# A two-layer decoder trunk on one core: the second layer's first gate moved into round 1, T's products put on both sides of the Gram products, and other moves of order

## The chip, the core and the metric

The kernel runs on one core of a Trainium2 chip. The core has a matrix engine (TensorE, PE), whose weight loads are listed apart (PEld), a vector engine (VectorE, DVE), a scalar engine (ScalarE, ACT), GpSimd (POOL) and SyncE (SP). Each runs its own program in order, and they wait for each other through semaphores. SP and POOL issue most of the DMA transfers, so a transfer that must wait for its buffer holds up those behind it on the same queue. The metric is the device time of one execution in microseconds.

## The reference

A 512 × 2048 fp32 input goes through two residual layers, each `x + W_out(mixer(RMSNorm(x)) * silu(gate))`.

Layer 0 is differential attention with 8 heads: `q, k, v, gate = split(h @ w_in)`; q and k are normalised and rotated; two softmax maps are subtracted (`a = p0 - lam * p1`); `o = a @ v` is normalised, gated and projected.

Layer 1 is RWKV-7 with 32 heads of 64 channels. A projection, mixed with its shift by one token, gives r, k, v, the gate and two low-rank terms for decay and learning rate. Each head then runs the scan

```
sa = S @ a_t
S  = S * w_t + sa b_t^T + v_t k_t^T
y  = S @ r_t
```

and y is normalised per head, gets a bonus term, is gated and projected.

## The kernel before

All large products are made from fp32r pairs: a float is split into a high and a low part (`split_w`: ACT casts the high part wh at L105, DVE subtracts to get the low part wl at L106), and each product is three matmuls (hH·wh, hL·wh, hH·wl). A unit of 48 such matmuls projects one block of columns. Almost all of PE's time is in these units (tile pp).

**Layer 0.** Head 0 uses `unit_tok`, heads 1 to 7 `unit_head`, a scheme with sums of blocks as in Strassen's method. The sums of weights are made by the DMA: `add_w` (L83) loads a weight block into a tile that holds another and adds it, on POOL's queue. The groups S1, S2, S3, S4 are products with sums of the activations; `all_groups` walks through one of them, splits each weight tile (wraw, or Ta to Td), issues its matmuls, and asks for the next sum in the same tile. b22 are the weight tiles that S4 loads and S3 uses; in the last head they are loaded in `third`, behind S2. Attention for head h−1 is a `Chain`: a generator of small steps that moves on by "ticks", one for each projection product issued. So its score, value and transposing products (sc, o, yt at L391) lie between head h's projections. The constants of layer 1 (`rwkv_consts`) are a chain too, put behind head 1, ahead of the attention chain in head 2. Then the out-projection follows, two column blocks by `unit_tok`, the rest by sums.

**Layer 1.** There are 16 rounds j, each for 128 channels (two heads). A round has units for k (with stage1), r (stage2), v (stage_v) and, from round 3, the gate of round j−3 (`LAG = 3`). Time is cut into 8 chunks of 64 tokens. In each round:

- `gram` (L1279) forms the products between keys and receptances of each chunk (gp, L1290), copies them to G on ACT (L1297), sums squares over channels (L1209, L1210, copy ssl at L1302), and sends both to DRAM (ltd, L1304 and L1310, on SP). `mask_gram` masks G on POOL.
- `t_solve` (L1335) loads them back as LT (POOL's queue, L1344), solves a triangular system in 31 pairs of DVE steps (L1355, L1357, end L1358), and writes td (L1359, SP).
- The chain of round j−1 runs among the units of round j. `t_combine` (L1366) loads TT from td (L1372), transposes it on DVE (T, L1382), and makes two products, px(T,G) (L1388) and, with the copy X between them (L1391), px(TT,X) (L1398). `scan_pair` then goes through the 8 chunks, with three dependent products each (sm at L1469, L1480, L1487) and copies on ACT between them (rhs L1472, VS L1482). After them come the outputs Y (L1509, L1513) and their centring.
- Later rounds finish: group norm, bonus, gate.

How far apart a chain's steps lie is written by hand in ticks: `GAP_D`, `GAP_X`, `GAP_T` in `t_combine`, and `gap`, `gap_s` in `scan_pair`. In round j > 2 `gram` moves the chain on by one step (`before.step`) right behind its own products. The rest of the order comes from a scheduler which sorts each engine's instructions by priorities (`AHEAD`, `SCAN`, `SOLVE` are offsets). After round 15 the last chain runs among the gates 13, 14, 15 and the out-projection of layer 1.

Of the kernel before, what the change touches and what calls it, by code (L numbers as in the profile page):

```python
# [82 lines left out]
def add_w(g, raw, part, k0):  # L83

    w, c = part
    g.nc.gpsimd.dma_start(out=raw[:], in_=w[c][:, k0 : k0 + KG], accum_op=ALU.add)

# [75 lines left out]
def unit_tok(g, aH, aL, parts, cols, npp=NT, more=None, late=True, turn=None, behind=None):  # L163

    nc = g.nc
    pts = [g.pp.tile([P, 512], F32, name="pp", tag="pp") if t < npp else
           g.ps.tile([P, 512], F32, name="pt", tag="pb", bufs=2) for t in range(NT)]
# [363 lines left out]
def unit_head(g, aps, h, t1s, sq, turned):  # L531
# [39 lines left out]

    def all_groups(out, lhs, raw, start=False, end=False, then=None):
        for i in range(N):
            r = raw(i)
            products(out, lhs(i), r, start and i == 0, end and i == N - 1)
            if then:
                add_w(g, r, then[0], then[1] + i * KG)

# [32 lines left out]
    def third():  # L611
        for i in range(N):
            if last:
                with g.tc.issue_after(behind):
                    b22.append(load(i, NH4, c2))
                add_w(g, b22[i], c2, i * KG)
            products(y, form("S3", i), b22[i], end=i == N - 1)
# [178 lines left out]
def layer0(g, aps):  # L796
# [3 lines left out]
    with ExitStack() as cx:  # L800
# [91 lines left out]
        for h in range(NH):  # L892
# [13 lines left out]
            if h:  # L906
                values = unit_head(g, aps, h, t1s, sq, lambda: Chain(g, keys(2), 9))
            else:
# [15 lines left out]
            if h == 1:  # L924
                Chain(g, rwkv_consts(g, aps))
                g.chains[0].step(g)
        rows = []
        for k in range(KT - 2):
            rows.append([g.hp.tile([P, T], F32R, name=n, tag=n) for n in ("hH", "hL")])
            for x, d in zip(rows[k], g.ys):  # L930
                nc.sync.dma_start(out=x[:].bitcast(F32), in_=d[k * P : (k + 1) * P, :])
        ch = Chain(g, attention(g, h, *before, 20, rows, rest), 16)
# [9 lines left out]
        def new_x(cb):  # L942
            xq = g.work.tile([P, NT, 512], F32, name="xq", tag=("sA", "sB", "qkL", "qkT")[cb], bufs=1)
            for t in range(NT):
                (nc.gpsimd if cb < 2 else nc.sync).dma_start(out=xq[:, t, :], in_=aps["x"][0, t * P : (t + 1) * P, cb * 512 : cb * 512 + 512])
            xs.append(xq)
            return xq
# [245 lines left out]

LAG = 3

# [83 lines left out]
def gram(g, j, p, before):  # L1279

    nc, w, BK = g.nc, g.work, p.BK
    p.G = w.tile([P, NC_, 2, 2, C], F32, name="G1", tag="G1", bufs=2)
    p.BKT = w.tile([P, NC_, P], F32, name="BKT", tag="BKT", bufs=2)
# [11 lines left out]
    for c0, gp in halves:  # L1295
        for h in range(2):
            nc.scalar.copy(p.G[:, c0 : c0 + 4, :, h, :], gp[h][:].rearrange("p (u x t) -> p u x t", u=4, x=2))  # L1297
    ps = g.ps.tile([P, 512], F32, name="pt", tag="pb", bufs=2)
    sum_channels(g, ps[:2, :], g.ones[:, 0 : P : C], p.k2)
    ss = w.tile([2, T], F32, name="ssl", tag="thg", bufs=1)  # L1300
    with g.tc.high_priority(offset=SOLVE if j == D // P - 1 else 0):
        nc.scalar.copy(ss[:], ps[:2, :])  # L1302
        for half in range(2):
            nc.sync.dma_start(  # L1304
                out=g.ltd[j % 2, half, :, :, HALF, :],
                in_=ss[:].rearrange("h (c b t) -> h c b t", c=NC_, b=2)[:, :, half, :])
        for half in range(2):
# [54 lines left out]

GAP_D, GAP_X, GAP_T = 18, 19, 8


def t_combine(g, j, p):  # L1366

# [9 lines left out]
    px = g.ps.tile([P, 512], F32, name="px", tag="pd", bufs=1)  # L1377
    yield GAP_D - GAP_T
    for h in range(2):
# [68 lines left out]

def chain(g, j, p, delay, gap, gap_s, others=()):
    def steps():  # L1450
        yield from t_combine(g, j, p)
        yield from scan_pair(g, j, p, gap, gap_s, dict(others))
# [100 lines left out]
def layer1(g, aps):  # L1553
    nc, tc = g.nc, g.tc
    with ExitStack() as cx:
# [17 lines left out]
        def receptances(j):  # L1573
            return shift_mix(g, proj(0, j), P, *mus(g, 0, j), "r", 1)

        begin(0)
# [43 lines left out]
        gps = proj(3, j - 1)  # L1620
# [139 lines left out]
```

## Time and profile before

| | |
|---|---|
| runs | 2126.84, 2135.11, 2135.95 us, median 2135.11 |
| the profiled execution | 2131.0 us, of which the span is 2129.3 |
| PE busy | 2091.2 us, 98% |
| DVE, ACT, POOL busy | 76%, 54%, 17% |
| mean granted PE clock | 0.996 |
| a steady round of layer 1 | 61.9 us |
| a steady head of layer 0 | 89.0 us |

The span is what the trace covers. A line of waits reads: engine, instruction and its line, what it waited for; total us, times, longest. A line of a timeline reads: start and length in us, engine, line, operation, tiles, shapes, count, and in brackets the idle time before it and what ended it. The granted clock is the share of its full rate at which the throttle let PE run.

### The profile page before, as it was taken

Reading aid. Unit: us, or ns where it says so; the run is one execution under the profiler, and the core shown is the slowest. Engines: PE = TensorE matmul, PEld = TensorE weight load, DVE = VectorE, ACT = ScalarE, POOL = GpSimd, SP = SyncE. Lnnn points to the kernel's source line nnn. Section 1 sums busy time; section 2 is a strip of 40 time slices with the busy share of each in tenths; the row PEclk is TensorE's granted clock in tenths of the full one; section 3 lists DMA queues with packets and bytes.
Section 4 is the critical chain, followed back from the end, with each engine's and each line's share of the span. In section 5 each row is a group of like instructions: output and inputs, shape, how many; then the busy total and the mean of one; then the engine's idle time right before and its main releaser. Section 6 shows DMA issues by size and latency. Waiting matters only on the chain.

```text
span 2129.3 us, 34082 instructions
## 1 busy us (share of the span) xinstructions
PE 2091.2 (98%) x11852; PEld 1690.3 (79%) x11852; DVE 1613.0 (76%) x4129; ACT 1155.5 (54%) x2278; POOL 367.9 (17%) x735
## 2 busy tenths in 40 slices
PE   9999999999999999999999999999999999999999
PEld 7888788888887788878677877778777777877787
DVE  6987888888888875576677777887777788776645
ACT  5765556566565543355555555555555555545322
POOL 1021111102113000101222221222222122231101
PEclk9999999999999999999999999999999999999999
DMA  8587878879789936722222332332333333345565
GB/s 266 161 166 186 161 167 186 164 189 172 178 183 215 314 113 179 150 90 88 78 74 84 98 91 84 93 91 77 94 103 88 84 91 92 107 134 178 173 171 121
DMA packets 158972, 294.60 MB, mean 138 GB/s; under 512 B 64352, under 2 KB 81760, under 8 KB 158800
## 3 DMA queue, kind: packets, MB, share of 16 engines
q1 hardware_dynamic: 109696, 182.82, 27.7%
q0 software_dynamic: 24448, 85.64, 22.0%
q10 hardware_dynamic: 24656, 23.97, 3.4%
q8 instruction: 93, 1.52, 0.3%
q14 instruction: 79, 0.65, 0.1%
HBM read 268.71 MB, written 23.66 MB: 137 GB/s over the span
## 4 chain that ended last, share of the span: by engine, by line
PE 77%; DVE 10%; ACT 6%; issue 3%; DMA 3%; ACTq 0%; POOL 0%; SPq 0%; DVEq 0%; POOLq 0%
PE pp L122 36%; PE pp L567 21%; PE pt L122 4%; DVE wl L106 3%; ACT wh L105 1%; PE gp L1290 1%; PE sc L122 1%; PE sm L1480 1%; PE sm L1469 1%; PE sm L1487 1%; PE o L122 1%; DVE tmpl L1355 1%; ACT VS L1427 1%; PE lora L122 1%; PE z L122 1%
## 5 line engine op out<-in xcount | busy, mean ns | idle before, releaser
L106 DVE TENSOR_TENSOR wl<-wraw,wh 128x1024 fp32r<-128x1024 f32 (+2 forms) x291 | 360.4, 1239 | 257.5 <-ACT wh L105 249.7
L105 ACT CAST wh<-wraw 128x1024 fp32r<-128x1024 f32 (+2 forms) x291 | 303.8, 1044 | 296.9 <-PE pp L122 130.3
L122 PE MATMUL pp<-hH,wl 128*128 128x512 f32 x1024 | 415.1, 405 | 0.0
L122 PE MATMUL pp<-hH,wh 128*128 128x512 f32 x1024 | 414.4, 405 | 0.0
L122 PE MATMUL pp<-hL,wh 128*128 128x512 f32 x1024 | 413.1, 403 | 0.0
L122 PEld LDWEIGHTS pp<-hH,wh 128*128 128x128 f32 x1024 | 193.7, 189 | 34.7 <-issue 0.6
L122 PEld LDWEIGHTS pp<-hL,wh 128*128 128x128 f32 x1024 | 193.9, 189 | 34.4
L122 PEld LDWEIGHTS pp<-hH,wl 128*128 128x128 f32 x1024 | 193.8, 189 | 34.0
L567 PE MATMUL pp<-wh,hH 128*128 128x512 f32 x448 | 177.8, 397 | 0.8 <-DVE G L528 0.8
L567 PE MATMUL pp<-wh,hL 128*128 128x512 f32 x448 | 176.8, 395 | 0.0
L122 PE MATMUL pp<-wh,hH 128*128 128x512 f32 x372 | 145.8, 392 | 3.9 <-ACT hH L1091 1.6
L122 PE MATMUL pp<-wl,hH 128*128 128x512 f32 x372 | 146.3, 393 | 0.4 <-DVE wl L106 0.4
L122 PE MATMUL pp<-wh,hL 128*128 128x512 f32 x372 | 146.0, 393 | 0.3 <-DVE hL L1092 0.2
L1355 DVE SCALAR_TENSOR_TENSOR tmpl<-LT,Tm 128x60 f32<-128x60 f32 (+24 forms) x496 | 134.7, 272 | 12.1
L567 PE MATMUL pp<-wl,hH 128*128 128x512 f32 x448 | 141.2, 394 | 1.3 <-DVE wl L106 1.3
L1475 POOL COPY SA<-VS 64x64 f32<-64x64 f32 x224 | 57.7, 257 | 466.6 <-DVE VS L1491 399.8
L1357 DVE TENSOR_TENSOR Tm<-Tm,tmpl 128x60 f32<-128x60 f32 (+24 forms) x496 | 103.6, 209 | 10.0 <-DVE tmpl L1355 0.2
L1472 ACT COPY rhs<-sm 64x64 f32<-64x64 f32 x256 | 53.0, 207 | 99.9 <-PE sm L1469 97.4
L567 PEld LDWEIGHTS pp<-wl,hH 128*128 128x128 f32 x448 | 84.8, 190 | 19.4 <-DVE wl L106 2.1
L567 PEld LDWEIGHTS pp<-wh,hH 128*128 128x128 f32 x448 | 84.7, 189 | 18.6 <-DVE G L528 1.2
L567 PEld LDWEIGHTS pp<-wh,hL 128*128 128x128 f32 x448 | 84.8, 189 | 16.4
L122 PEld LDWEIGHTS pp<-wh,hH 128*128 128x128 f32 x372 | 69.9, 188 | 19.6 <-ACT hH L1091 2.6
(393 smaller groups left out, 4426.5 us busy)
## 6 DMA issues: line engine op xcount, KB each, us to landing
wraw<-in_rw_w_in_dram SPq DMA_DIRECT2D x128, 512.0 KB, 3.9
wraw<-in_da_w_in_dram SPq DMA_DIRECT2D x75, 512.0 KB, 3.5
wraw<-in_da_w_in_dram POOLq DMA_DIRECT2D x28, 512.0 KB, 6.1
wraw<-in_da_w_out_dram SPq DMA_DIRECT2D x26, 512.0 KB, 4.5
wraw<-in_rw_w_out_dram SPq DMA_DIRECT2D x26, 512.0 KB, 4.5
Ta<-in_da_w_in_dram POOLq DMA_DIRECT2D x21, 512.0 KB, 5.9
Tb<-in_da_w_in_dram POOLq DMA_DIRECT2D x21, 512.0 KB, 5.8
Tc<-in_da_w_in_dram POOLq DMA_DIRECT2D x21, 512.0 KB, 5.8
```

What stands on the lines that cost most here:

```text
L105: a = nc.scalar.copy(hi[:, ks], raw[:, ks])
L106: d = nc.vector.tensor_sub(lo[:, ks], raw[:, ks], hi[:, ks].bitcast(F32))
L122: m = nc.tensor.matmul(out, a, b, start=s, stop=e, skip_group_check=skip)
L567: m = nc.tensor.matmul(out[t][:], x, wt[lo][:, k, :], start=first, stop=end and lo == 1 and k == KG - 1, skip_group_check=True)
L1290: m = nc.tensor.matmul(gp[h][:, i * P : (i + 1) * P], BK[r_, c0 + i, :, :], p.AR[r_, c0 + i, :, :], start=True, stop=True)
L1355: nc.vector.scalar_tensor_tensor(tt, LT[:, i : i + 1, i + 1 :].to_broadcast([P, s, n]), n2[:, i : i + 1], Tm[:, 0:s, i : i + 1].to_broadca ...
L1357: nc.vector.tensor_add(Tm[:, 0:s, i + 1 :], Tm[:, 0:s, i + 1 :], tt)
L1427: nc.scalar.copy(p.VS[(1 - h) * C : (2 - h) * C, par : NC_ : 2, h, :], pv[par * C : par * C + C, :, h, :])
L1469: nc.tensor.matmul(sm[:, 0:P], both(p.G[:, c, 0]), both(VS[:, c]), start=True, stop=True)
L1472: nc.scalar.copy(rhs[r_, :], sm[r_, h * C : h * C + C])
L1475: nc.gpsimd.tensor_copy(p.SA[r_, c - 1, :], VS[r_, c, h, :])
L1480: nc.tensor.matmul(sm[:, P : P + C], both(g.TT[j % 2][:, c]), rhs[:], start=True, stop=True)
```

## The change

1. `LAG` goes from 3 to 2. Gate 0 is computed in round 1, in a tile of its own (tag g0), and applied at the end of round 2; later gates come one round sooner; after the loop gates 14 and 15 are left.
2. In `gram` the channel sums, their copy and their two transfers go ahead of the Gram products, with the `SOLVE` offset in every round, and in another bank.
3. `GAP_X` goes from 19 to 10. From round 4 on, with `before.step` from j > LAG + 1, T's first product stands ahead of the Gram products and its second behind them. The first three rounds have leads of their own (54, 28, 18 ticks), and the scan's gaps there change. The last chain starts after 24 ticks, not 66, with a lead of 20.
4. In the last attention head b22's loads and adds are asked for right behind the adds that follow S1's groups (these make the weights of S2), and the adds that follow S2's groups come behind those of b22; the chain of keys starts after 16 ticks there, not 9.
5. `rwkv_consts` runs in one go behind head 1 and not as a chain.
6. The loads of xq for the out-projection all go on SP, behind the last load of ys.
7. In `unit_tok` with fewer pp banks, tiles 0 and 3, not 0 and 1, take them.

The number of instructions of each kind stays, but for the eight xq loads that go from POOL to SP. The program of changed orders shows how the points come out: in head 2 the attention products stand 424 PE instructions ahead of those of head 3, as in the heads after it; in rounds 4 to 15 PE goes Y, 32 projection matmuls, px(T,G), the sums, the Gram products, px(TT,X), 8 projection matmuls, the first scan product, and ACT goes G, X, ssl, X, G, sHx, four G, two TT, the square ysq, a cast wh, two rhs; on POOL's queue the four adds that make S2's weights stand ahead of b22's four.

```diff
 def unit_tok(...):
-    pts = [... name="pp", tag="pp") if t < npp else
+    pts = [... name="pp", tag="pp") if npp == NT or t % 3 == 0 else
...
-    all_groups(X, lambda i: form("S1", i), chained, True, last, (c2, NH4))
+    added = all_groups(X, lambda i: form("S1", i), chained, True, last, (c2, NH4))
     copy_out(g, acc[2:], X)
     b22 = []
-    if not last:
+    if last:
+        for i in range(N):
+            b22.append(load(i, NH4, c2))
+            with g.tc.issue_after(added):
+                added = add_w(g, b22[i], c2, i * KG)
+    else:
...
-    all_groups(y, lambda i: form("S2", i), chained, then=(c1, NH4))
-    behind = g.m.ins
+    all_groups(y, lambda i: form("S2", i), chained, then=(c1, NH4), added=last and added)
...
             if h == 1:
-                Chain(g, rwkv_consts(g, aps))
-                g.chains[0].step(g)
+                for _ in rwkv_consts(g, aps):
+                    pass
...
-            for t in range(NT):
-                (nc.gpsimd if cb < 2 else nc.sync).dma_start(out=xq[:, t, :], ...)
+            with tc.issue_after(loaded):
+                for t in range(NT):
+                    nc.sync.dma_start(out=xq[:, t, :], ...)
...
-LAG = 3
+LAG = 2
...
 def gram(g, j, p, before):
+    ps = g.ps.tile([P, 512], F32, name="pt", tag="pa", bufs=1)
+    sum_channels(g, ps[:2, :], g.ones[:, 0 : P : C], p.k2)
+    ...
...
-GAP_D, GAP_X, GAP_T = 18, 19, 8
+GAP_D, GAP_X, GAP_T = 18, 10, 8
...
-    yield GAP_D - GAP_T
+    yield lead
...
-                full = LAG <= j < D // P - 1
-                gaps = (6, 8 if j > LAG else 7) if full else (4, 5) if j > 1 else (3, 4)
-                chain(g, j - 1, pairs[j - 1], 5, *gaps, others).step(g)
-                if j == 1:
-                    pairs[0].chain.wait += 34
+                full = LAG < j < D // P - 1
+                gaps = ((6, 8) if j > LAG + 1 else (5, 6)) if full else (5, 5) if j == 1 else (4, 5)
+                leads = {1: 54, LAG: 28, LAG + 1: 18}
+                chain(g, j - 1, pairs[j - 1], 5, *gaps, others, leads.get(j, GAP_D - GAP_T)).step(g)
...
-                    gram(g, j, p, j > 2 and pairs[j - 1].chain)
+                    gram(g, j, p, j > LAG + 1 and pairs[j - 1].chain)
...
-                if j == 2:
-                    pairs[1].chain.wait = 16
...
+            if j == 1:
+                first = gate_of(0, "g0")
...
-            if j >= LAG:
-                gated(g, j - LAG, pairs[j - LAG], gate(g, j - LAG, proj(3, j - LAG)))
+            if j > LAG:
+                gated(g, j - LAG, pairs[j - LAG], gate_of(j - LAG))
...
+            if j == LAG:
+                gated(g, 0, pairs[0], first)
-        chain(g, j, p, 66, 5, 6)
-        gated(g, j - 2, pairs[j - 2], gate(g, j - 2, proj(3, j - 2)))
+        chain(g, j, p, 24, 5, 6, lead=20)
...
-        gts.append(gate(g, j, proj(3, j, behind=(24, last_but_one)), "E"))
+        gts.append(gate(g, j, proj(3, j, behind=(15, last_but_one)), "E"))
...
-            if n >= KT and len(rows) < KT:
+            if n >= KT - 2 and len(rows) == KT - 1:
```

More of the change, by code (lines that the diff above doesn't have):

```diff
@@ L85, in add_w @@
     w, c = part
-    g.nc.gpsimd.dma_start(out=raw[:], in_=w[c][:, k0 : k0 + KG], accum_op=ALU.add)
+    return g.nc.gpsimd.dma_start(out=raw[:], in_=w[c][:, k0 : k0 + KG], accum_op=ALU.add).ins
 @urgent
@@ L165, in unit_tok @@
     nc = g.nc
-    pts = [g.pp.tile([P, 512], F32, name="pp", tag="pp") if t < npp else
+    pts = [g.pp.tile([P, 512], F32, name="pp", tag="pp") if npp == NT or t % 3 == 0 else
            g.ps.tile([P, 512], F32, name="pt", tag="pb", bufs=2) for t in range(NT)]
@@ L570, in products, with all_groups @@
                         first = False
-    def all_groups(out, lhs, raw, start=False, end=False, then=None):
+    def all_groups(out, lhs, raw, start=False, end=False, then=None, added=None):
         for i in range(N):
@@ L576, in all_groups @@
             if then:
-                add_w(g, r, then[0], then[1] + i * KG)
+                with g.tc.issue_after(added) if added else ExitStack():
+                    added = add_w(g, r, then[0], then[1] + i * KG)
+        return then and added
     def s4(out, keep, start=False, end=False):
@@ L612, in third @@
         for i in range(N):
[L613 to L616, printed above, removed]
             products(y, form("S3", i), b22[i], end=i == N - 1)
@@ L930, in layer0 @@
             for x, d in zip(rows[k], g.ys):
-                nc.sync.dma_start(out=x[:].bitcast(F32), in_=d[k * P : (k + 1) * P, :])
+                loaded = nc.sync.dma_start(out=x[:].bitcast(F32), in_=d[k * P : (k + 1) * P, :]).ins
         ch = Chain(g, attention(g, h, *before, 20, rows, rest), 16)
@@ L943, in new_x @@
             xq = g.work.tile([P, NT, 512], F32, name="xq", tag=("sA", "sB", "qkL", "qkT")[cb], bufs=1)
-            for t in range(NT):
-                (nc.gpsimd if cb < 2 else nc.sync).dma_start(out=xq[:, t, :], in_=aps["x"][0, t * P : (t + 1) * P, cb * 512 : cb * 512 + 512])
+            with tc.issue_after(loaded):
+                for t in range(NT):
+                    nc.sync.dma_start(out=xq[:, t, :], in_=aps["x"][0, t * P : (t + 1) * P, cb * 512 : cb * 512 + 512])
             xs.append(xq)
@@ L1281, in gram @@
     nc, w, BK = g.nc, g.work, p.BK
+    ps = g.ps.tile([P, 512], F32, name="pt", tag="pa", bufs=1)
+    sum_channels(g, ps[:2, :], g.ones[:, 0 : P : C], p.k2)
+    ss = w.tile([2, T], F32, name="ssl", tag="thg", bufs=1)
+    with g.tc.high_priority(offset=SOLVE):
+        nc.scalar.copy(ss[:], ps[:2, :])
+        for half in range(2):
+            nc.sync.dma_start(
+                out=g.ltd[j % 2, half, :, :, HALF, :],
+                in_=ss[:].rearrange("h (c b t) -> h c b t", c=NC_, b=2)[:, :, half, :])
     p.G = w.tile([P, NC_, 2, 2, C], F32, name="G1", tag="G1", bufs=2)
@@ L1297, in gram @@
             nc.scalar.copy(p.G[:, c0 : c0 + 4, :, h, :], gp[h][:].rearrange("p (u x t) -> p u x t", u=4, x=2))
-    ps = g.ps.tile([P, 512], F32, name="pt", tag="pb", bufs=2)
-    sum_channels(g, ps[:2, :], g.ones[:, 0 : P : C], p.k2)
-    ss = w.tile([2, T], F32, name="ssl", tag="thg", bufs=1)
     with g.tc.high_priority(offset=SOLVE if j == D // P - 1 else 0):
[L1302 to L1306, printed above, removed]
         for half in range(2):
@@ L1360, in t_solve, with t_combine @@
     return ld.ins
-GAP_D, GAP_X, GAP_T = 18, 19, 8
-def t_combine(g, j, p):
+GAP_D, GAP_X, GAP_T = 18, 10, 8
+def t_combine(g, j, p, lead):
     nc, w, TT = g.nc, g.work, g.TT[j % 2]
@@ L1446, with chain @@
 HEADS = ((0, slice(0, C)), (1, slice(C, P)))
-def chain(g, j, p, delay, gap, gap_s, others=()):
+def chain(g, j, p, delay, gap, gap_s, others=(), lead=GAP_D - GAP_T):
     def steps():
-        yield from t_combine(g, j, p)
+        yield from t_combine(g, j, p, lead)
         yield from scan_pair(g, j, p, gap, gap_s, dict(others))
@@ L1574, in receptances, with gate_of @@
             return shift_mix(g, proj(0, j), P, *mus(g, 0, j), "r", 1)
+        def gate_of(i, tag="v", **k):
+            return gate(g, i, proj(3, i, **k), tag)
         begin(0)
```

2 lines of the change are left out of this document (1 added, 1 removed).

## The prediction

> **What bounds the kernel.** I read the page's first and fourth parts, then what TensorE (PE) waited for, then stretches of the span, then the timelines round the long waits.
>
> ```profile
> span 2129.3 us, 34082 instructions
> ...
> PE 2091.2 (98%) x11852; PEld 1690.3 (79%) x11852; DVE 1613.0 (76%) x4129; ACT 1155.5 (54%) x2278; POOL 367.9 (17%) x735
> ...
> PE 77%; DVE 10%; ACT 6%; issue 3%; DMA 3%; ACTq 0%; POOL 0%; SPq 0%; DVEq 0%; POOLq 0%
> ```
>
> PE is busy for 2091.2 of 2129.3 us. The change neither adds nor removes a matmul, so the time can move only by the 38.1 us in which PE is idle, by new idle time, and by time at a reduced clock, which counts as busy. The waits of PE, then one table of stretches (columns: length; busy time and instructions of PE, weight loads, DVE, ACT, POOL; granted PE clock; DMA share; GB/s):
>
> ```profile
> PE sm L1480 <- ACT rhs L1472: 4.7, 12, 0.7
> PE yt L391 <- DVE y L382: 3.9, 2, 3.4
> PE px L1388 <- DVE T L1382: 3.3, 2, 3.2
> ...
> PE px L1388 <- DVE y L1550: 1.6, 1, 1.6
> ...
> PE pp L567 <- ACT wh L105: 1.1, 2, 0.7
> ```
> ```profile
> 204.00:300.00 96.00, 91.77 (x427) 75.28 (x426) 76.50 (x201) 55.23 (x98) 14.02 (x17) 0.96 0.76 164
> 389.00:478.00 89.00, 88.96 (x427) 73.51 (x426) 77.27 (x201) 54.51 (x98) 13.63 (x16) 1.00 0.82 178
> 257.80:264.60 6.80, 5.87 (x15) 4.40 (x16) 4.72 (x21) 3.97 (x10) 0.00 (x0) 0.50 0.33 108
> 667.00:674.00 7.00, 5.77 (x24) 3.56 (x23) 4.66 (x14) 4.75 (x10) 0.85 (x1) 1.00 1.06 202
> 1032.60:1042.80 10.20, 10.20 (x68) 7.79 (x67) 1.23 (x1) 3.72 (x9) 1.30 (x2) 0.50 0.45 135
> 1052.00:1075.00 23.00, 22.27 (x152) 15.18 (x150) 20.48 (x61) 13.50 (x39) 7.96 (x16) 1.00 0.22 70
> 1094.00:1126.00 32.00, 31.02 (x156) 23.75 (x155) 26.26 (x77) 20.88 (x54) 9.42 (x22) 1.00 0.15 47
> 1444.75:1506.60 61.85, 61.28 (x421) 49.02 (x421) 47.30 (x130) 35.01 (x79) 14.06 (x35) 1.00 0.31 90
> 1936.00:1950.00 14.00, 11.03 (x79) 8.63 (x77) 12.99 (x21) 12.12 (x21) 0.00 (x0) 1.00 0.78 242
> ```
>
> Only two waits are long, 3.4 us in head 2 and 3.2 us in round 1, and behind each the clock stands at 0.50: for 6.80 and for 10.20 us. The wait of 1.6 us in the tail leaves it at 1.00. So a wait of about 3 us costs twice: itself, and half of the slow stretch, 3.4 and 5.1 us. The other idle time is crumbs: 0.57 us in a steady round of 61.85.
>
> **Head 2.** Heads 2 and 4 issue the same 427 matmuls, in 96.00 and 89.00 us. In head 2 the attention chain stands behind the 18 steps of the constants' chain, so its products fall elsewhere among the projections, and one of them (yt) meets a DVE that is still busy. The change runs the constants inline behind head 1; in the changed program each attention product of head 2 stands where it stands in heads 3 to 6, which have no such wait. I take the whole difference: 96.00 − 89.00 = **−7.0 us**. Bounds: −8 if the 0.9 us at head 2's start, where a weight split stood behind the constants on DVE, goes too; 0 if the wait only moves. The constants themselves are the same instructions.
>
> **Head 7.** Now the four accumulating loads of b22 go ahead of, and between, the adds that make S2's weights on POOL's queue; S2's first groups then wait for their weights: the stretch 667 to 674 has 7.00 − 5.77 = 1.23 us of idle time, and the waits name wh at L105 (1.1 us). The change puts the adds for S2 first. I take **−1.5 us**; bounds −3 (all the idle time of this head and the out-projection that could hang on it) and +1. Eight xq loads move from POOL to SP, four of them per column block, between weight loads; SP is a queue that waits in order, so this is where +1 comes from. The banks' new order in unit_tok costs nothing: it only chooses which two of four tiles sit in which pool.
>
> **Round 1 of layer 1.** T(0) is made by a chain of steps:
>
> ```profile
> 981.52 0.43 SPq L1310 DMA_DIRECT2D ltd<-G  x1
> ...
> 992.48 1.23 DVE L106 TENSOR_TENSOR wl<-wraw,wh 128x1024 fp32r<-128x1024 f32 x1 [4.92 <-ACT wh L105]
> 993.62 0.17 DVE L1346 TENSOR_SCALAR LT<-LT 128x32 f32<-128x32 f32 x1
> ...
> 1023.87 0.42 DVE L1358 TENSOR_TENSOR Tm<-Tm,LT 128x256 f32<-128x256 f32 x1
> ...
> 1024.45 0.39 SPq L1359 DMA_DIRECT2D td<-Tm  x1
> ...
> 1028.84 1.79 SPq L1372 DMA_DIRECT2D TT<-td  x4
> ...
> 1031.70 0.44 DVE L1382 STREAM_TRANSPOSE T<-TT 64x256 f32<-64x256 f32 x1 [0.67 <-DMA TT<-td]
> ```
>
> The channel sums and their copy now go ahead of the Gram products, and on SP the six ltd transfers go without a weight load between them: the last leaves at about 979.8 instead of 981.5. On DVE the solve no longer stands behind the split at 992.48 (it comes inside the solve), so it starts at about 990.1 instead of 993.6. One split is added within it and one moved behind it, 1.2 us each, so its 30.7 us stay and it ends near 1020.9 rather than 1024.3. The way out stays 4.4 us for td (1024.45 to 1028.84). But SP now has a weight load ahead of TT that waits for a split until about 1025.7, so TT leaves near 1026.1, 2.7 us sooner. A 0.74 us mix operation stands between the two transposes now, and both halves of T's first product follow each other. They stand at the same place in PE's program as before, so I expect a wait of 1.2 us (0 to 2) instead of 3.2, and no slow stretch, since 1.6 us left the clock alone: −2.0 − 5.1 = **−7.1 us**. Bounds: −8.3, and 0 if the wait stays near 3.
>
> [...]
>
> **Scan gaps of rounds 1 and 2.** The scan's steps stood 3 and 4 (4 and 5 in round 2) products apart, now 5 and 5 (4 and 5), with the first gate's 48 products moved into round 1. The idle time of the two stretches is 0.73 + 0.98 = 1.7 us. I take **−1.5 us**; bounds −1.7 and +1. The moved unit is the same work earlier, so zero, with the tail losing its cover (below).
>
> **Rounds 4 to 15.** Here the order of T's products and the Gram products changes, and it costs. Rows of a steady round of before, PE and ACT:
>
> ```profile
> 1441.11 2.06 PE L1290 MATMUL gp<-AR,BK 64*128 64x128 f32 x32
> 1443.10 1.09 PE L1388 MATMUL px<-T,G 32*32 32x32 f32 x32
> 1444.12 0.40 PE L1209 MATMUL pt<-sHx,ones 128*2 128x512 f32 x1
> ...
> 1452.00 0.38 PE L1469 MATMUL sm<-VS,G 128*128 128x128 f32 x2
> ```
> ```profile
> 1442.30 1.56 ACT L1297 COPY G<-gp 128x512 f32<-128x512 f32 x3 [5.39 <-PE gp L1290]
> 1443.82 0.62 ACT L1394 COPY G<-AR 64x512 f32<-64x512 f32 x1
> 1444.45 0.74 ACT L1391 COPY X<-px 32x256 f32<-32x256 f32 x2
> ...
> 1446.47 1.05 ACT L105 CAST wh<-wraw 128x1024 fp32r<-128x1024 f32 x1
> 1447.43 0.61 ACT L1100 CAST sHx<-mixr 128x512 fp32r<-128x512 f32 x1
> 1447.94 0.57 ACT L1302 COPY ssl<-pt 2x512 f32<-2x512 f32 x1
> 1450.16 0.74 ACT L1401 COPY TT<-px 32x256 f32<-32x256 f32 x2 [1.64 <-PE px L1398]
> 1452.42 0.42 ACT L1472 COPY rhs<-sm 64x64 f32<-64x64 f32 x2 [1.52 <-PE sm L1469]
> ```
>
> Before, PE goes 13 projection matmuls behind Y, Gram, px(T,G), sums, 19 matmuls, px(TT,X), and ACT is idle 1.64 and 1.52 us on the way to the scan. After, all of it stands in one block: 32 matmuls, px(T,G), sums, Gram, px(TT,X), 8 matmuls, the first sm, 6 matmuls, the second sm (L1480). From px's start P that is 1.02 + 0.47 + 1.99 + 1.02 + 8 × 0.23 + 0.13 + 6 × 0.23 = 7.9 us. ACT in the changed order has, between P + 0.7 and the second sm: two G<-AR of 0.63, two X of 0.37, ssl and sHx at 0.51, four G<-gp at 0.52, two TT at 0.37, a square of 0.63 (L1535), a wh cast of 0.96 and two rhs of 0.21: 7.7 us, so it is ready at P + 8.4, and with the durations above in place of the spacings at P + 9.1. So the second sm waits 0.5 to 1.2 us in each of 12 rounds, less what a steady round already waits at L1480 (4.7 us over all rounds). I take 0.6 us a round, **+7 us**; bounds 0 (the 0.57 us idle of a round goes at the same time) and +12. px(TT,X) itself wants X at P + 3.5, and the copies end at P + 2.7, so it doesn't wait. T is no problem by the same rows: Gram comes about 5.9 us later in the round, and so does the next px.
>
> **The tail.** The last round's rows:
>
> ```profile
> 1893.77 0.18 DVE L1346 TENSOR_SCALAR LT<-LT 128x32 f32<-128x32 f32 x1
> ...
> 1922.35 0.38 SPq L1359 DMA_DIRECT2D td<-Tm  x1
> ...
> 1930.81 1.80 SPq L1372 DMA_DIRECT2D TT<-td  x4
> ...
> 1934.43 0.44 DVE L1382 STREAM_TRANSPOSE T<-TT 64x256 f32<-64x256 f32 x1
> ```
>
> One gate unit fewer stands ahead of the last chain: px(15) comes 257 instructions behind Gram(15) instead of 319, about 50 us instead of 62.6. T(15) took 17.3 us to the solve, 28.5 us for it, 8.5 us for td, 3.6 us to the second transpose: 58. With ssl sooner (−1.5), and td at 4.4 us as in round 1, because the loads that crowd it now start some 7 us before it, 52. A wait of 1.5 to 2 us, then, where 1.6 stood: **0 us**. Bounds: −3 (this wait and others of the tail gone), +9 (td still 8.5 us long: a wait of 5.5 us and a slow stretch of 5.1).
>
> **Sum.** −7.0 − 1.5 − 7.1 − 1.5 + 7 + 0 = −10.1 us, from the profiled execution's 2131.0 us: **2121 us**. The median shown is 2135.11, 4.1 us above that execution, so 2121 is 0.66% under the median. About 0.5%, 10.7 us, is what a measurement here can tell from no change.
>
> **Rivals.** *ACT keeps up.* The scheduler's block is hidden: the rounds cost 0 to 2 us, the rest as above: 2113 us. For it: ACT is 54% busy. Against: the order on ACT puts a square and a cast ahead of rhs. Chance 0.20.
>
> *The long waits stay* (the change doesn't do what it says): head 2's wait or the px wait in round 1 stays over about 3 us with its slow stretch, or the tail gets one: 2128 us with one of them (2121 + 7), 2135 with two. For it: round 1's T gains only 2 to 3 us, with SP still serving a load ahead of TT; and the tail has lost 12 us of cover. Against: the orders of head 2 equal those of heads without a wait. Chance 0.23.
>
> *T becomes late in every steady round*, and the kernel slower. In the round of the last table T went out so:
>
> ```profile
> 1498.48 1.83 SPq L1372 DMA_DIRECT2D TT<-td  x4
> ```
>
> px followed at 1443.10 + 61.85 = 1505.0, 2.4 us later if 32 and not 13 matmuls and Gram lie between Y and px: 1507.4. The last ltd transfer would leave some 2 us later against the scan (Gram 5.9 us later, but ssl, which left last, first), TT near 1500.5, and landed and transposed as in round 1 (1028.84 to 1032.1) T is there at 1503.8: a margin of 3.6 us. If td or TT then stands behind a weight load on SP, or the transposes behind the centring of Y on DVE, for 5.6 us, px waits 2 us in each of 12 rounds: +24, 2145 us. It decides from 4.4 us of lateness (0.8 us a round takes the gain back). For it: SP's order changes all through the round. Against: the margin. Chance 0.10.
>
> **How the numbers follow.** The forecast (2115 to 2126) has 0.47; ACT keeping up 0.20; long waits staying 0.23; late T 0.10. The range 2110 to 2136 leaves out part of the first rival and the last. Faster by over 0.5% (under about 2124.4) takes the second case and most of the first: 0.58. Within 0.5% takes the third and the rest: 0.32. Slower: 0.10.
>
> **What would show it.** Right: head 2 in 89 us at clock 1.00; no 0.50 behind px in round 1; waits of sm L1480 on rhs L1472 at some 7 to 12 us instead of 4.7, one per steady round at the first step, and a round of about 62.4 us; idle time at 667 to 674 gone. Wrong: a px wait on T in steady rounds, a 0.50 clock in the tail, or a steady round that keeps 61.9 us.

## The result

The changed kernel takes 2119.9 us (median of 7 runs, 2115.9 to 2121.7) against 2133.9 us before (7 runs, 2126.8 to 2136.0): a ratio of 0.994, 95% interval 0.9925 to 0.9956. The forecast was 2121 us. The profiled execution took 2118.3 us, its span 2116.6 us, 12.7 us under the one of before. Of all executions in this document one, of experiment 4, took 2258.0 us at a granted clock of 0.85 where the others had 0.99 or more; the median given below is that of the other nine.

The total came out right, but not by the terms of the sum. Three came out worse than forecast, and the largest cost came out as a gain. First the page of the changed kernel, then the waits of PE:

```profile
span 2116.6 us, 34038 instructions
...
PE 2079.7 (98%) x11852; PEld 1690.7 (80%) x11852; DVE 1607.8 (76%) x4129; ACT 1155.7 (55%) x2278; POOL 360.9 (17%) x727
```
```profile
PE pt L363 <- DVE rs_i L65: 7.0, 1, 7.0
PE sm L1484 <- ACT rhs L1476: 6.5, 15, 0.9
PE sm L1491 <- ACT VS L1486: 4.0, 14, 0.5
PE px L1392 <- DVE y L1416: 2.0, 1, 2.0
...
PE px L1392 <- DVE y L1554: 1.7, 1, 1.7
PE px L1392 <- DVE T L1386: 1.5, 1, 1.5
```

(Lines of layer 1 have moved by 3 to 4: L1484 is the second scan product, L1480 before; L1392 is px(T,G), L1388 before; L1402 is px(TT,X), L1398 before.) The wait of 3.4 us in head 2 is gone. In its place stands one of 7.0 us in head 7 that was not there before. px waits for over a microsecond three times instead of twice; the rows name DVE's y for two of the three, and not T, which the part on round 1 comes back to. The stretches of the changed kernel, with the same columns as before:

```profile
202.29:291.24 88.95, 88.87 (x426) 73.38 (x425) 77.66 (x203) 54.13 (x96) 13.59 (x16) 1.00 0.81 178
380.11:469.01 88.90, 88.82 (x426) 73.31 (x424) 77.15 (x201) 54.45 (x97) 13.63 (x16) 1.00 0.81 178
664.00:686.00 22.00, 16.88 (x85) 13.85 (x83) 13.72 (x47) 10.86 (x24) 7.80 (x9) 0.97 1.06 208
684.50:691.30 6.80, 3.46 (x10) 2.90 (x11) 3.87 (x17) 1.53 (x2) 0.00 (x0) 0.50 1.01 208
1025.80:1029.20 3.40, 3.40 (x27) 2.36 (x26) 0.07 (x1) 2.77 (x5) 1.42 (x2) 0.50 0.24 73
1135.10:1138.50 3.40, 3.40 (x21) 2.36 (x22) 2.90 (x13) 0.58 (x1) 0.00 (x0) 0.50 0.68 181
1498.00:1559.57 61.57, 60.78 (x422) 49.17 (x421) 46.79 (x131) 34.96 (x78) 14.58 (x35) 1.00 0.31 90
1930.40:1937.20 6.80, 6.80 (x46) 5.31 (x45) 3.81 (x7) 4.84 (x10) 0.00 (x0) 0.50 0.66 224
```

Head 2 and head 4 now take the same time (first two rows). A steady round (rounds 5 to 14) takes 61.57 us, not 61.85 to 61.95: shorter, where the prediction had it longer. Round 4, the first in the new order, takes 62.2. There are four slow stretches at a clock of 0.50 where there were two: one from inside the 7.0 us wait on, and one behind each of the three waits of px, though these are only 1.5 to 2.0 us long.

Both programs issue the same matmuls, and in layer 0 in the same number between any two places, so the time from the n-th to the m-th matmul can be compared directly. In layer 1 the places move against each other, so there the rounds are compared from Y to Y, and the first rounds are what is left.

| part | before, us | after, us | difference | forecast |
|---|---|---|---|---|
| start to the end of head 1 | 200.1 | 198.1 | −2.0 | (0 to −1) |
| head 2 | 95.8 | 88.9 | −6.8 | −7.0 |
| heads 3 to 6 | 355.9 | 355.5 | −0.4 | 0 |
| head 7 and start of the out-projection | 85.1 | 88.4 | +3.3 | −1.5 |
| rest of layer 0, start of layer 1, to px(TT,X) of round 1 | | | −3.1 | −7.1 |
| rest of rounds 1 to 4 (what is left of the sum) | | | about −3.5 | −1.5 |
| steady rounds, 10 × 0.34 | | | −3.4 | +7 |
| last round and tail (waits and slow time over the usual spacing) | 15.1 | 18.4 | +3.3 | 0 |

### The profile page after: what moved, and what is told of

It is laid out like the page before. It is cut to its first block, busy times and chain, and to the rows that moved or that the text cites. A ratio compares the mean times of both kernels' runs of the same rounds, so it can differ in the third digit from the quotient of the medians.

```text
span 2116.6 us, 34038 instructions
## 1 busy us (share of the span) xinstructions
PE 2079.7 (98%) x11852; PEld 1690.7 (80%) x11852; DVE 1607.8 (76%) x4129; ACT 1155.7 (55%) x2278; POOL 360.9 (17%) x727
## 4 chain that ended last, share of the span: by engine, by line
PE 79%; DVE 11%; ACT 5%; DMA 2%; issue 2%; ACTq 0%; SPq 0%; DVEq 0%
PE pp L122 39%; PE pp L567 21%; PE pt L122 5%; DVE wl L106 2%; ACT wh L105 1%; PE sc L122 1%; PE sm L1473 1%; PE o L122 1%; PE sm L1491 1%; DVE tmpl L1359 1%; PE sm L1484 1%; DVE Tm L1361 1%; PE gp L1302 1%; PE lora L122 1%; PE z L122 1%
## 5 line engine op out<-in xcount | busy, mean ns | idle before, releaser
L1479 POOL COPY SA<-VS 64x64 f32<-64x64 f32 x224 | 67.7, 302 | 443.8 <-DVE VS L1495 390.2
```

What stands on the lines that cost most here:

```text
L1479: nc.gpsimd.tensor_copy(p.SA[r_, c - 1, :], VS[r_, c, h, :])
```

## The experiments

Theory after the result: (a) head 2 is worth what it seemed; (b) the 7.0 us wait in head 7 is made by the new place of b22's adds; (c) in steady rounds the predicted wait at the scan's second product is there, but the new order saved more than it cost; (d) the three waits of px are real lateness of T, and waits as short as these (1.5 to 2.0 us) are followed by a slow clock. The rivals stand in the expectations. The kernel before took 2131.2 to 2133.4 us (medians) beside the experiments and 2133.9 beside the changed kernel, so a difference from the changed kernel is also given by the two ratios to the kernel before (their difference times 2133.9 us).

### The burst of adds in head 7

Where the 7.0 us come from can be followed in the timelines of the changed kernel, POOL's queue first, then the stores on ACT's queue, DVE, and PE:

```profile
664.54 3.85 POOL L86 DMA_DIRECT2D wraw<-in_da_w_in_dram  x4
668.05 1.21 POOL L86 DMA_DIRECT2D Ta<-in_da_w_in_dram  x1
671.14 0.85 POOL L86 DMA_DIRECT2D Tb<-in_da_w_in_dram  x1 [1.88 <-DVE yTl L400]
```
```profile
671.46 0.71 ACTq L385 DMA_DIRECT2D ys<-yTl  x1
```
```profile
687.11 0.35 DVE L400 SCALAR_TENSOR_TENSOR yTl<-yt,subw,yTh 128x128 fp32r<-128x128 f32 x1 [8.11 <-DMA ys<-yTl]
```
```profile
687.84 0.47 PE L363 MATMUL pt<-ident,a 128*128 128x128 f32 x1 [6.96 <-DVE rs_i L65]
```

b22's four adds leave in one go at 664.54, straight behind Td's at 664.00, and Ta and Tb follow at 668.05 and 671.14. The DMA share of the stretch 664 to 686 is 1.06. A small store of the attention's output, issued at 671.46 in the midst of this, lands only at about 687.1, 15.6 us later; before, such stores took 1.9 to 5.8 us. DVE writes the next value into the same tile, so it waits 8.1 us, and with it everything behind it on DVE: the vector operations of the attention step and the weight splits. PE waits 7.0 us, and from 684.50 on the clock is at 0.50 for 6.8 us; PE is busy for only 3.46 us of that, so the slow clock adds an estimated 1.7 us, half of it. Experiment 1 moves the four adds behind those that follow S2's groups:

```diff
     if last:
         for i in range(N):
             b22.append(load(i, NH4, c2))
-            with g.tc.issue_after(added):
-                added = add_w(g, b22[i], c2, i * KG)
...
-    all_groups(y, lambda i: form("S2", i), chained, then=(c1, NH4), added=last and added)
+    added = all_groups(y, lambda i: form("S2", i), chained, then=(c1, NH4), added=last and added)
     if last:
+        for i in range(N):
+            with g.tc.issue_after(added):
+                added = add_w(g, b22[i], c2, i * KG)
```

> The changed kernel with one thing moved: b22's four adds in head 7 come behind the adds that follow S2's groups, not ahead of them. Theory (a burst of accumulating loads fills the DMA engines, so the store of yTl lands late and PE waits 7.0 us for what stands behind yTl on DVE): the wait of pt L363 and the slow stretch behind it go, 7.1 + 3.4 us, and S3 may wait up to 3 us for b22: 2108 to 2111 us against the changed kernel's 2118.3. Rival (the later start of the chain of keys, or the xq loads on SP, make the wait): it stays, 2118.

Measured: 2112.95 us (2109.9 to 2115.5), 7.0 us under the changed kernel's 2119.9 (7.7 by the ratios). The wait of pt L363 and the slow stretch behind it are gone. Head 7 from the 3014th to the 3400th matmul takes 83.7 us, not 88.4. b22 is 2.3 us late for S3 (the last 150 of these matmuls take 35.35 us, not 33.03), which the expectation had allowed for. The late keys and xq on SP are still in this kernel, so they don't make the wait.

Experiment 2 puts the function of the heads and the chain of keys back whole:

```diff
-    if last:
-        for i in range(N):
-            b22.append(load(i, NH4, c2))
-            with g.tc.issue_after(added):
-                added = add_w(g, b22[i], c2, i * KG)
-    else:
+    if not last:
...
-    all_groups(y, lambda i: form("S2", i), chained, then=(c1, NH4), added=last and added)
+    all_groups(y, lambda i: form("S2", i), chained, then=(c1, NH4))
+    behind = g.m.ins
...
+            if last:
+                with g.tc.issue_after(behind):
+                    b22.append(load(i, NH4, c2))
+                add_w(g, b22[i], c2, i * KG)
...
-                values = unit_head(g, aps, h, t1s, sq, lambda: Chain(g, keys(2), 9 if h < NH - 1 else 16))
+                values = unit_head(g, aps, h, t1s, sq, lambda: Chain(g, keys(2), 9))
```

> The changed kernel with head 7's order of adds and its chain of keys as in the kernel before; xq still on SP. Theory: no 7.0 us wait, but S2's waits of before come back; head 7 as a whole cost 3.4 us from 3014 to 4500 instructions of PE, so about 2115 us against 2118.3. Rival (xq on SP or the constants' place causes the wait): 2118 to 2121.

Measured: 2112.63 us (2111.7 to 2114.9), 7.3 us faster than with the change, more than the 3.4 expected. The expectation took head 7 as it was before, but xq stays on SP here, and the stretch behind S2 took 30.0 us, not 32.4. S2's own stretch shows what the new order of the adds was worth: 19.6 us with the old order, 16.8 with the new one, so 2.3 to 2.9 us. Undone alone, this part of the change would have made the kernel faster by about 7 us; the part is a loss on balance. Whether xq's queue alone gives the 2.5 us in the next stretch was not tried apart.

### The constants and head 2

```diff
-                for _ in rwkv_consts(g, aps):
-                    pass
+                Chain(g, rwkv_consts(g, aps))
+                g.chains[0].step(g)
```

> The changed kernel with the constants of layer 1 as a chain again. Theory (the place of head 2's attention products alone makes its wait and slow stretch): head 2 takes 96 us again, and the split behind the constants waits 0.9: 2118.3 + 7 to 8 = 2125 to 2126 us. Rival (the constants' chain does not matter by itself): 2118.

Measured: 2127.46 us (10 runs, 2123.8 to 2131.9), 7.6 us above the changed kernel (7.3 by the ratios). The old wait is back with its old length, and head 2 takes 95.95 us (88.95 in the changed kernel). Waits of PE in this kernel, 200 to 300 us:

```profile
PE yt L391 <- DVE y L382: 3.4, 1, 3.4
PE pp L567 <- DVE G L528: 0.9, 1, 0.9
PE pp L567 <- DVE wl L106: 0.8, 1, 0.8
```

The third line, a weight split behind the constants on DVE, is the 0.9 us that the prediction held open. Theory (a) stands.

### Layer 1 apart

Layer 1 of the kernel before (`LAG`, `gram`, the gaps, `t_combine`, `chain` and the rounds of `layer1`) behind layer 0 of the changed one; the core of the edit:

```diff
-LAG = 2
+LAG = 3
...
-GAP_D, GAP_X, GAP_T = 18, 10, 8
+GAP_D, GAP_X, GAP_T = 18, 19, 8
...
-                    gram(g, j, p, j > LAG + 1 and pairs[j - 1].chain)
+                    gram(g, j, p, j > 2 and pairs[j - 1].chain)
...
-        chain(g, j, p, 24, 5, 6, lead=20)
+        chain(g, j, p, 66, 5, 6)
```

> Layer 0 as in the changed kernel, layer 1 as in the kernel before. The traces put 5.8 us of the gain of 12.7 in layer 0 and 6.9 in layer 1. Theory (the two add up): 2131.0 - 5.8 = 2125 us. Rival (layer 1's reordering gives nothing by itself, its difference is chance of the slow stretches): 2118 to 2120.

Measured: 2126.46 us against 2132.65 of the kernel before (ratio 0.9973, 0.9962 to 0.9984): by the ratio −5.8 us, as the 5.8 of layer 0 had it. The other 7 us of the gain are layer 1's. The two add up.

### The steady rounds

The prediction said that the scan's second product would wait for ACT in every steady round. The timeline of ACT in the changed kernel has the order that it worked out, and its time between the two that it gave: px starts at 1438.0, so the last copy, rhs, ends at P + 8.8, where P + 8.4 and P + 9.1 stood:

```profile
1438.74 0.62 ACT L1398 COPY G<-AR 64x512 f32<-64x512 f32 x1 [3.15 <-PE px L1392]
...
1442.05 2.06 ACT L1309 COPY G<-gp 128x512 f32<-128x512 f32 x4
1443.97 0.74 ACT L1405 COPY TT<-px 32x256 f32<-32x256 f32 x2
1444.74 0.63 ACT L1539 ACTIVATE ysq<-yc 128x512 f32<-128x512 f32 x1
1445.28 1.04 ACT L105 CAST wh<-wraw 128x1024 fp32r<-128x1024 f32 x1
1446.34 0.43 ACT L1476 COPY rhs<-sm 64x64 f32<-64x64 f32 x2
```
```profile
1446.82 0.43 PE L1484 MATMUL sm<-rhs,TT 128*128 128x64 f32 x2 [0.48 <-ACT rhs L1476]
```

Counted from start to start, the product comes 0.65 us later than it would without the wait (0.88 us behind the matmul ahead of it, where an undisturbed one comes 0.23 behind). So that term was right, 0.6 us a round; PE would have come to the product at P + 8.15, not 7.9. What was missed is on the other side. Summed by kinds of steps over nine rounds, the new order has one turn fewer between projections and other products: before, PE turns from projections to Gram, from Gram to px(T,G), and from projections to px(TT,X), after it turns to px(T,G) and goes through the whole block; that saves 0.22 us a round. And of the small waits of the scan that a round had before, 1.5 us start to start, the one at the fourth chunk (0.51) and most of the others are gone; without the new first one they come to about 0.65. Experiment 5 moves the scan's first product three matmuls later, to take the new wait away alone:

```diff
-    yield GAP_T
+    yield GAP_T + (3 if 3 <= j < D // P - 1 else 0)
```

(the last yield of `t_combine`; j is the pair there, so the edit reaches rounds 4 to 15)

> The changed kernel with the scan's first product three projection matmuls later in rounds 4 to 14. Theory (ACT's chain of copies behind T's products is ready 0.64 us after the second product of the scan is wanted, a fixed lateness): three matmuls, 0.69 us, take that wait away in 11 rounds, a steady round falls from 61.57 to 60.9 us, the kernel by 7 to 2113 us against the median 2119.9. Rival (ACT's work is conserved and the wait comes out at a later step of the same round): a steady round stays within 0.2 us of 61.57, 2118 to 2121.

Measured: 2110.12 us (2107.5 to 2112.1), 9.8 us under the changed kernel (7.9 by the ratios); the two intervals against before, 0.9887 to 0.9919 and 0.9925 to 0.9956, don't meet. A steady round takes 60.77 us, and the wait does not come out elsewhere in it:

```profile
1500.00:1560.77 60.77, 60.54 (x426) 49.46 (x424) 46.49 (x130) 34.57 (x79) 16.27 (x35) 1.00 0.31 92
```

PE is idle for 0.23 us of it, 0.79 us in the changed kernel. So the wait was real, it was a fixed lateness, and without it the new order is worth 1.1 us a round. Only in the last round, which the edit reaches too, does a wait come out behind it: 2.4 us at the transposes of the centred Y (L1552), where the changed kernel waits 0.3.

Experiment 9 asks whether the order alone does it, or the earlier gates. It is the kernel before with the changed kernel's `gram` and:

```diff
-GAP_D, GAP_X, GAP_T = 18, 19, 8
+GAP_D, GAP_X, GAP_T = 18, 10, 8
...
-                    gram(g, j, p, j > 2 and pairs[j - 1].chain)
+                    gram(g, j, p, j > LAG and pairs[j - 1].chain)
```

> The kernel before, with the new gram (sums first), GAP_X of 10 and T's first product ahead of Gram from round 4, and nothing else: gates still three rounds later, the first rounds' and the last chain's waits as they were. Theory (the order in a steady round alone makes the difference of 0.34 us a round, whatever the gates do): a steady round of 61.57 instead of 61.9, 11 rounds, so about 4 us under the kernel before (2127 against 2131), give or take slow stretches; GAP_X also shortens the first rounds' chains, which may add a wait there. Rival (the earlier gates give the rounds their gain): a steady round of 61.9 or more; with the first step's wait added as the prediction had it, 62.5.

Measured: 2128.63 us against 2133.44 in the same runs (ratio 0.9982, 0.9970 to 0.9993): −4.8 us, and 61.53 us for a steady round. The order makes the difference in a steady round, and the gates' rounds have no part in it.

Experiment 8 puts the sums and ssl behind the Gram products again, in the changed kernel:

```diff
 def gram(g, j, p, before):
-    ps = g.ps.tile([P, 512], F32, name="pt", tag="pa", bufs=1)
-    sum_channels(g, ps[:2, :], g.ones[:, 0 : P : C], p.k2)
...
     for c0, gp in halves:
         for h in range(2):
             nc.scalar.copy(p.G[:, c0 : c0 + 4, :, h, :], gp[h][:].rearrange("p (u x t) -> p u x t", u=4, x=2))
+    ps = g.ps.tile([P, 512], F32, name="pt", tag="pb", bufs=2)
+    sum_channels(g, ps[:2, :], g.ones[:, 0 : P : C], p.k2)
...
```

> The changed kernel with the channel sums, their copy and transfers behind the Gram products again. The order of ACT before the scan's second product then lacks the square. Theory (the block of T's products and Gram saves the turns of PE between kinds of products, and the sums' place only sets ACT's order and T's start): the first scan step's wait of 0.64 falls by about 0.5, a steady round to 61.1 to 61.4 us, but T(0) and T(2) start about 1.5 us later and the waits of px in rounds 1 and 3 grow by that: 2116 to 2121. Rival (the early sums are what made the rounds shorter): a steady round of 61.8 to 62, 2124 us or more.

Measured: 2120.1 us, as the changed kernel (2.6 us more by the ratios, but the intervals overlap: 0.9937 to 0.9967 against 0.9925 to 0.9956). Nine of the ten steady rounds take 60.7 to 61.3 us, shorter still than expected, since the square now stands behind rhs on ACT. But T is late in six rounds, the first, the third, the last, and three from round 4 on:

```profile
PE px L1392 <- DVE T L1386: 9.5, 7, 3.0
```

In round 8 the waits are 1.7 us and the round takes 62.9; in round 4 the wait is 1.2 us, a slow stretch of 6.8 us follows at 1195, and the round takes 66.9; in round 12 it is 0.2 us. In the tail 2.6 us of wait are followed by 13.6 us at half clock. So the third rival of the prediction, T late in the steady rounds, comes in part in a kernel that lacks the early sums: with them no px from round 4 to round 14 waits for T. They pay for this with the square's place ahead of rhs.

### The leads

```diff
-                leads = {1: 54, LAG: 28, LAG + 1: 18}
+                leads = {1: 66, LAG: 28, LAG + 1: 26}
...
-        chain(g, j, p, 24, 5, 6, lead=20)
+        chain(g, j, p, 34, 5, 6, lead=30)
```

> The changed kernel with longer leads ahead of T's products in rounds 1 (54 to 66 ticks) and 3 (18 to 26) and in the last chain (24 and 20 to 34 and 30). Theory (T is 2.1, 1.6 and 1.7 us late there, and each lateness costs its slow stretch too, 1.7 + 1.7 + 3.4): the three waits of px and their stretches go, 2108 us against 2119.9; if part of a wait stays, the slow stretch may stay with it, 2113. Rival (the scans, squeezed by the later start, give it back in waits at sm and at the end of the round): 2117 to 2121.

Measured: 2112.89 us (2111.1 to 2116.0), −7.0 us (−5.5 by the ratios). Of the waits of px(T,G), two of 0.7 us and less are left in rounds 1 to 3, both of them for y (L1416) and not for T, and no slow stretch stands behind them; none is left in the tail. The gain is under the 12 us that the waits and stretches sum up to; what kept the rest was not followed up, but behind waits of px of about this length in the kernels before and after (1.48, 1.61 and 1.65 us) the clock stood at 0.50 for 3.41, 0 and 6.83 us, so their full price was too much to expect of a median.

### Together

Experiment 7 has the adds of experiment 1, the later scan of experiment 5 and the leads of experiment 6.

> The changed kernel with b22's adds behind, the scan's first product three matmuls later, and the longer leads. If the three add up: 2119.9 - 7.0 (measured) - 7 - 8 to 12 = 2094 to 2098 us. If the scan's wait only moves: 2101 to 2105. If the leads are given back too: 2112.

Measured: 2102.55 us (2101.1 to 2104.3), ratio to before 0.9869, 0.9854 to 0.9883. That is 15.2 us less than the changed kernel by the ratios, where the three differences (7.7, 7.9 and 5.5 by the ratios) come to 21.1; where the other 6 us went was not followed up. The rounds are as in experiment 5, 60.75 us, and all but one of the slow stretches are gone; the last round waits 2.0 us at the transposes of the centred Y (L1553), as in experiment 5, with the one slow stretch left:

```profile
PE sm L1474 <- DVE VS L1496: 4.1, 16, 0.7
PE pt L1553 <- DVE yc L1546: 2.0, 1, 2.0
```

Experiment 10 has head 7 of the kernel before in place of the adds behind.

> As the three together (2102.6), with head 7's adds and keys as in the kernel before in place of the adds behind. From the stretches of PE's program 3014 to 3400 in two runs (83.7 us with the adds behind, 82.7 with the old order and xq on SP) it should be 1 us faster: 2101.5. If the store's wait comes back: 2108 or more.

Measured: 2102.91 us (2101.0 to 2104.3), the same. Head 7's stretch is 83.3 us here, 83.7 there: the two ways to place the adds cannot be told apart. Either is 15 to 17 us faster than the changed kernel by the ratios, and 28 to 31 us faster than the kernel before.

## Why the prediction was right or wrong

**Head 2: right.** Forecast −7.0, with up to −8 together with the 0.9 us at its start. Measured −6.8, and 1.2 us at the end of head 1; undone, +7.6. Comparing a disturbed head with an undisturbed one of the same matmuls gave the wait and its slow stretch in one number.

**Head 7: wrong, +3.3 where −1.5 stood.** The mechanism that was priced came: S2's stretch got shorter by 2.3 us. The step that failed is the bound "+1", which was put down to the xq loads on SP. The work that the change moved, b22's four adds, was not costed at its new place: it was noted where they left, not what they would meet. Four adds of 512 KB in one go behind four others kept the DMA engines at 1.06 for 22 us, and a small store behind them held up DVE.

**Round 1: half, −3.1 where −7.1 stood.** px waited 2.0 us, against 3.2 before and 1.2 forecast. T itself came as late as forecast: px was due at 1022.39, and the second transpose ended at 1023.59, 1.2 us later. The rest of the wait is for another operation:

```profile
1023.15 0.44 DVE L1386 STREAM_TRANSPOSE T<-TT 64x256 f32<-64x256 f32 x1
1023.63 0.69 DVE L1416 TENSOR_TENSOR y<-pt,mixv 128x512 f32<-128x512 f32 x1
```
```profile
1024.38 1.09 PE L1392 MATMUL px<-T,G 32*32 32x32 f32 x32 [1.99 <-DVE y L1416]
```

In the program px and the pt that y reads have one tag, pd, with a single buffer, so px cannot be written before y has read pt. Before, this y stood on DVE ahead of the transposes (1026.51 against 1030.60); now it stands behind them, and px starts 0.06 us after its end. The prediction had no such step. That T came out at 1.2 is partly luck. TT did leave much earlier (1018.74, with the kernel 5.5 us ahead of the one before at that place: 4.6 us sooner against the matmuls, not 2.7). But its first part came on DVE only at 1022.05, 3.3 us after it was issued, not 1.8, and the mix operation stood between the two transposes, as foreseen. The second step that failed is "no slow stretch, since 1.6 us left the clock alone": a wait of 2.0 us was followed by 3.41 us at half clock. Term by term the wait fell by 1.2 us (forecast 2.0) and the price of the slow stretch by 3.4 (forecast 5.1), 4.6 together; the row of the table shows less because it is cut at px(TT,X), where the stretch of the kernel before still has 2 to 3 us to run.

**Scan gaps of the first rounds.** Forecast −1.5; what is left of the sum says about −3.5, of which about 1.2 belong to round 1's slow stretch, with a new wait of 1.5 us of px in round 3 (this one for T) and its slow stretch (1.7 us) inside it. Round 3's lead was not looked at in the prediction. Experiment 6 took that wait away.

**Steady rounds: the wait right, the sum wrong, −3.4 where +7 stood.** The failing step is "I take 0.6 us a round, +7 us": only the new wait was put in the sum. The old waits of the round were taken off as a bound, "the 0.57 us idle of a round goes at the same time", and not as part of the likeliest value; and the turns between kinds of products, which are not idle time in the profile, were not in it at all. A block that goes through in one piece saves 0.22 us of turns and 0.9 of waits and pays 0.65. (ACT's list adds up to 7.85 us, not 7.7, with both rhs in it, which changes little.) The chance of the rival "ACT keeps up" (0.20) was too low for a time of a round at or below the old one, though ACT did not keep up.

**Tail: forecast 0, measured +3.3.** The wait of px(15) was 1.65 us, as forecast (1.5 to 2), but that is luck: the reading of the wait before was wrong. It was not for T(15), which was there at 1934.87, 4.6 us before px was due at 1939.50; it was for the bank, as in round 1, which here the y of `finish_y` reads. Kernel before, then changed kernel:

```profile
1940.31 0.74 DVE L1550 SCALAR_TENSOR_TENSOR y<-pt,prm_hgw,y 128x512 f32<-128x512 f32 x1
```
```profile
1927.49 0.44 DVE L1386 STREAM_TRANSPOSE T<-TT 64x256 f32<-64x256 f32 x1
1927.96 0.75 DVE L1554 SCALAR_TENSOR_TENSOR y<-pt,prm_hgw,y 128x512 f32<-128x512 f32 x1
```

px started at 1941.11 and at 1928.77, each time 0.06 us after y. In the changed kernel T is 0.8 us late and y, behind it on DVE, makes up the rest. The wait was followed by 6.83 us at half clock, which the wait of 1.6 us in the kernel before was not; there the same step as in round 1 failed. But those 3.4 us are not the +3.3 of the table: from px(15) to PE's last product the two kernels take 183.8 and 183.5 us (for 918 and 914 products), since two waits of the kernel before (1.4 us for mixE, 0.9 for hH) are gone. Most of the loss lies ahead of px(15), in the last round, where 1.3 us of waits for rhs are new; the rest of it was not followed up.

**The total** was 2121 forecast and 2119.9 measured because errors cancel: −10.4 us in the steady rounds, about −2 in the first heads and −2 in the first rounds stand against +4.8 in head 7, +4.0 in round 1 and +3.3 in the last round and tail. By the prediction's own signs, head 2 came out right; a 0.50 behind px in round 1 and in the tail, waits for rhs of 6.5 us and not 7 to 12, and a round of 61.57 us and not 62.4 say that the rest did not. Of the rivals, "the long waits stay" happened in part, at a place that was not named for it.

## What to carry to other kernels

When transfers are moved, ask what small transfer shares the DMA engines at the new place, and who waits for it: four loads issued in one go cost 7 us here through a store of 128 KB that nobody had on the list. When a block of dependent steps is put together, count the waits and turns that it takes away as well as the one that it makes, and then move the consumer by the lateness that is left: three matmuls were worth 0.8 us in every round. When a product waits, read which operation the row names: twice here the wait ended not with the operand but with the reader of the bank that the product writes. And where a matrix engine is 98% busy, the waits that are left can be worth more than they look: here three of px, of 1.48 to 1.99 us, were followed by 3.41, 3.41 and 6.83 us at a clock of 0.50 (one of 1.61 us, in the kernel before, by none).

## What the runs showed of the hardware

These are the waits of PE of over 1 us in the profiled executions of the kernel before and of the changed one, from 12 us on, and the time at a clock of 0.50 behind each, from the records of the granted clock (the slow time at the end of each program is left out):

| kernel | product that waited | idle from, us | wait, us | clock at 0.50 from, us | for, us |
|---|---|---|---|---|---|
| before | yt, head 2 | 254.49 | 3.44 | 257.79 | 6.83 |
| before | px, round 1 | 1027.92 | 3.17 | 1032.61 | 10.24 |
| before | px, tail | 1939.49 | 1.61 | not at all | 0 |
| before | pp, tail | 1948.59 | 1.35 | not at all | 0 |
| changed | pt, head 7 | 680.88 | 6.96 | 684.50 | 6.83 |
| changed | px, round 1 | 1022.38 | 1.99 | 1025.83 | 3.41 |
| changed | px, round 3 | 1132.86 | 1.48 | 1135.06 | 3.41 |
| changed | px, tail | 1927.11 | 1.65 | 1930.37 | 6.83 |

The lengths are one, two or three times 3.41 us. The starts lie 227 times 3.413 us apart in the kernel before, and 100, 32 and 233 times in the changed one. In the stretch in the tail of the changed kernel the projection matmuls from 1933.58 us on follow each other at 0.43 us from start to start, and behind it, from 1937.32 on, at 0.23.

So neither the start nor the length of a slow stretch follows from the length of the wait alone. A wait of 1.61 us was followed by none, one of 1.65 us by 6.83 us, and one of 1.48 us by 3.41. The wait of px in round 1 of layer 1 as it was before, 3.1 to 3.2 us, was followed by 10.24 us at half clock in the kernel before and by 3.41 in experiment 4:

```profile
1026.40:1029.81 3.41, 3.41 (x16) 2.40 (x12) 0.44 (x1) 0.70 (x2) 2.36 (x4) 0.50 1.01 256
```

What decides it was not shown. For a forecast the price of the clock is therefore still a chance: here an estimated 0, 1.7, 3.4 or 5.1 us (half of the time at 0.50), for waits of 1.48, 1.61 and 1.65 us and for two of 3.1 to 3.2 us.
